# Causal attention in groups of four query tiles: values over up to 512 columns, a written TensorE order, value halves added on GpSimd

## The chip, the core and the metric

One core of a Trainium2 chip runs the whole program; the other cores are idle. The metric is the device time of one execution in microseconds (us), and lower is better. A time is the median over several executions.

Engines are named as in the profile: PE is TensorE (matmuls and transposes), PEld its weight loads, DVE is VectorE, ACT is ScalarE, POOL is GpSimd, SP is the engine that issues DMAs. Each takes its instructions in the order in which they stand in its own queue, and waits on semaphores that other engines raise.

## The reference

The program is one layer of a decoder: a gated feed-forward half step, three mixing branches, an output projection, and a second feed-forward half step, over 1024 tokens of width 1024 in float32. Only the middle branch is touched, a causal attention with 8 heads, queries and keys of 96 features (64 plain and 32 rotated) and values of 64:

```python
def causal_block_attention(q, k, v):              # q, k: (1, 1024, 8, 96), v: (1, 1024, 8, 64)
    ...
    def one_block(args):                          # Q_BLOCK = 128 queries at a time
        i, qi = args
        s = jnp.einsum('bqhd,bkhd->bhqk', qi, k).astype(jnp.float32) * scale
        qpos = i * Q_BLOCK + jnp.arange(Q_BLOCK)
        mask = kpos[None, :] <= qpos[:, None]
        s = jnp.where(mask[None, None], s, NEG)
        p = jax.nn.softmax(s, axis=-1)
        return jnp.einsum('bhqk,bkhd->bqhd', p.astype(v.dtype), v)
```

## The kernel before

Products are made from float32 values that are kept as two parts, a high part (`hi`, fp32r) and a rest (`lo`). `split` makes them: ACT copies the value to `hi` (L139), then DVE subtracts `hi` from the value to get `lo` (L142). `mm3` (L155) multiplies two such pairs with three matmuls (L158, L159, L160).

`attention` (L941) works on tiles of 128 queries by 128 keys. Head `h` has 8 query tiles, taken in four steps `j` of two tiles (`t` = 0, 1). Four kinds of work make a head:

- `prepare(h)` brings queries and keys to a layout with features on the partitions: four transposes of 128x96 (L450) into one PSUM bank, then ACT with a gain (L150) and DVE for the rest (L151). Four such pieces a head are spread over the steps of the head before.
- `scores(h, j)`: for each of two query tiles, three matmuls for each 512 columns of keys into a PSUM tile `mm` (two of these exist, of two banks each); DVE adds the causal mask and takes the row's extreme in one instruction (L1001, followed by a small read of the accumulator), writing the tile `pr0` to `pr7` that belongs to the query tile; ACT takes the exponential and its row sum (L1007).
- `turn(h, j)`: PE transposes the 128x128 blocks of `pr` (L1023) into a bank, four to a bank, and `split` makes `whi` and `wlo` from the bank. Blocks above the diagonal that a value product needs are cleared by POOL (L1028).
- `value(h, j)`: for each block row of keys `kk`, two matmuls over 256 columns (L1039 with `whi`, L1040 with `wlo`) into one bank. The stationary operand is `vv[kk]`, which holds the 64 high and the 64 low columns of the values side by side, so the bank's upper 64 rows and lower 64 rows are two halves of the result that have to be added: ACT copies one half (L1047), DVE adds the other (L1048) into `ysum`.

After two heads a 512-column piece of `ysum` is complete. The row sums' reciprocals (L1051) go to DRAM and come back spread over 64 partitions (L1066, L1068), POOL multiplies (L1071), and `split` writes the result to `yt` for the branch product that follows. For the last head PE transposes do that spreading instead of the DMAs (L1061).

The loop over steps runs `scores` of step n, then `turn` of step n-1, then `value` of step n-2. No order is written by hand in this stage: a scheduler puts the recorded instructions on each engine's queue. There are four PSUM banks of 512 columns (`bank`) for transposes and value sums together; `wide` tiles (`whi`, `wlo`) have five buffers each. `products` are matmuls of another branch that fill the start of the stage.

Of the kernel before, what the change touches and what calls it, by code (L numbers as in the profile page):

```python
# [8 lines left out]
F32 = mybir.dt.float32  # L9
# [4 lines left out]
ALU = mybir.AluOpType  # L14
AXX = mybir.AxisListType.X

P = 128
# [32 lines left out]
class Kernel:  # L50
# [890 lines left out]
    def attention(self, products):  # L941
# [16 lines left out]
        yt, st, qkt, pair, ysum, inv, late = [], {}, {}, {}, {}, {}, []  # L958
        sums = self.dram.tile([H // 2, 2, 2, 4 * P], F32, name="invd")
        with tc.tile_pool(name="att", bufs=1) as p:  # L960
# [21 lines left out]
            def scores(h, j):  # L982
                qt, kt = qkt[h]
                prs = []
                if h % 2 == 0 and j == 0:
                    inv[h // 2] = self.small.tile([P, 2, NT], F32, name="a_rs", tag="a_rs")
                rs = inv[h // 2][:, h % 2, 2 * j:2 * j + 2]
                mx, = (self.stat(x, 2) for x in ("a_mx",))
                ns = []
                for t in range(2):  # L990
                    i = 2 * j + t
                    n = {0: 256, 4: 768}.get(i, (i + 1) * P)
                    sc = self.mm().rearrange("p a b -> p (a b)")
                    for c0 in range(0, n, 512):
                        c = slice(c0, min(n, c0 + 512))
                        self.mm3(
                            sc[:, c], tuple(x[:, i * P:(i + 1) * P] for x in qt),
                            tuple(x[:, c] for x in kt), True, True)
                    pr = p.tile([P, (i + 1) * P], F32, name=f"pr{i}", bufs=1)
                    m, m0 = (i + 1) * P, (NT - 1 - i) * P  # L1000
                    nc.vector.tensor_tensor_reduce(  # L1001
                        out=pr[:, :m], in0=sc[:, :m], in1=self.mask[:, m0:m0 + m], scale=1.0, scalar=-NEG,
                        op0=ALU.add, op1=ALU.min, accum_out=mx[:, t:t + 1])
                    ns.append(m)
                    prs.append(pr)
                for t, (pr, n) in enumerate(zip(prs, ns)):
                    nc.scalar.activation(  # L1007
                        pr[:, :n], pr[:, :n], ACT.Exp, bias=mx[:, t:t + 1], scale=-1.0, accum_out=rs[:, t:t + 1])
                st[h, j] = prs

            def turn(h, j):
                prs, out = st[h, j], []
# [1331 lines left out]
```

## Time and profile before

| | |
|---|---|
| median of 3 runs | 2162.41 us (2160.59 to 2163.39) |
| the profiled execution | 2161.68 us, of which the span of its instructions is 2160.0 us |
| PE, PEld, DVE, ACT, POOL busy, whole span | 100%, 83%, 73%, 42%, 12% |
| granted PE clock | 1.00 |
| the attention stage, about 1240 to 1400 us | of 160 us PE is busy 158.59, DVE 138.78, ACT 130.61, POOL 28.04 |
| DMA in that stretch | 0.25 of its time, 78 GB/s |

Matmuls are pipelined: the profile gives one a duration that reaches into the next, so the busy share of PE hides short waits, and the cost of a matmul in a stream is read from start to start. On the other engines an instruction's start to the next one's start is also a little less than its duration, where they follow without a wait.

### The profile page before, as it was taken

To read this page: it belongs to the slowest core of one execution; us is meant where nothing else is said; L and a number is where in the kernel's file an instruction comes from. 1 tells how busy PE (TensorE), PEld (TensorE's weight loads), DVE (VectorE), ACT (ScalarE), POOL (GpSimd) and SP (SyncE) were. 2 spreads that over 40 slices of the span, in tenths; PEclk is the share of its full clock that TensorE was granted. 3 is DMA by queue.
4 is the path that set the end of the run, shared out by engine and by line. 5 is a ranking of instruction groups with operands and counts; after the bars stand their busy time and mean duration, and the time that the engine had idled before them with its cause. 6 is when DMAs were issued, how large, how long until landed. Compare 5 with 4: busy or idle time off the path is not lost.

```text
span 2160.0 us, 27488 instructions
## 1 busy us (share of the span) xinstructions
PE 2150.9 (100%) x10112; PEld 1797.1 (83%) x10112; DVE 1568.7 (73%) x2370; ACT 909.4 (42%) x1485; POOL 253.2 (12%) x256
## 2 busy tenths in 40 slices
PE   9999999999999999999999999999999999999999
PEld 6888888888888888888888899888888888888887
DVE  8966666679889657654886689886876666657884
ACT  6433333343455334433555378733433223224332
POOL 0011111100000000000123311230011212110000
PEclk9999999999999999999999999999999999999999
DMA  4264555585344444641687832292133332347543
GB/s 148 93 221 166 183 178 205 178 320 193 119 134 156 147 161 176 215 149 61 221 284 255 315 100 71 79 348 101 40 127 103 112 98 99 103 146 287 168 129 104
DMA packets 139751, 350.44 MB, mean 162 GB/s; under 512 B 21984, under 2 KB 30304, under 8 KB 139616
## 3 DMA queue, kind: packets, MB, share of 16 engines
q1 hardware_dynamic: 139472, 348.68, 46.9%
q8 instruction: 79, 1.29, 0.2%
q14 instruction: 56, 0.46, 0.1%
q10 hardware_dynamic: 144, 0.00, 0.0%
HBM read 235.62 MB, written 113.01 MB: 161 GB/s over the span
## 4 chain that ended last, share of the span: by engine, by line
PE 93%; DVE 4%; ACT 1%; DMA 1%; issue 0%; SPq 0%; POOL 0%; ACTq 0%; DVEq 0%; POOLq 0%
PE one L158 15%; PE one L159 15%; PE one L160 15%; PE bank L159 13%; PE bank L158 13%; PE bank L160 13%; PE mm L158 1%; PE mm L159 1%; PE mm L160 1%; PE bank L1023 1%; PE one L1979 1%; PE bank L1039 1%; DVE pr L1001 1%; PE bank L1040 1%; PE bank L1979 0%; DMA whi<-wks 0%
## 5 line engine op out<-in xcount | busy, mean ns | idle before, releaser
L146 ACT CAST whi<-x 128x1024 fp32r<-128x1024 f32 x202 | 192.2, 954 | 405.6 <-DVE x L1449 160.8
L147 DVE TENSOR_TENSOR wlo<-x,whi 128x1024 fp32r<-128x1024 f32 x202 | 237.3, 1176 | 70.1 <-DMA wkv<-wlo 24.6
L1483 DVE TENSOR_TENSOR t<-t,one 128x512 f32<-128x512 f32 x188 | 129.0, 686 | 184.7 <-PE one L160 182.3
L158 PE MATMUL bank<-h,whi 128*128 128x512 f32 x636 | 248.0, 390 | 0.0
L160 PE MATMUL bank<-h,wlo 128*128 128x512 f32 x636 | 247.7, 389 | 0.0
L159 PE MATMUL bank<-h,whi 128*128 128x512 f32 x636 | 247.6, 389 | 0.0
L158 PE MATMUL one<-h,whi 128*128 128x512 f32 x508 | 198.5, 391 | 0.0
L160 PE MATMUL one<-h,wlo 128*128 128x512 f32 x508 | 197.7, 389 | 0.0
L159 PE MATMUL one<-h,whi 128*128 128x512 f32 x508 | 197.7, 389 | 0.0
L158 PE MATMUL one<-w,whi 128*128 128x512 f32 x432 | 168.7, 391 | 0.2 <-DVE t L1483 0.2
L160 PE MATMUL one<-w,wlo 128*128 128x512 f32 x432 | 168.2, 389 | 0.0
L159 PE MATMUL one<-w,whi 128*128 128x512 f32 x432 | 168.2, 389 | 0.0
L142 DVE TENSOR_TENSOR wlo<-w,whi 128x1024 fp32r<-128x1024 f32 (+2 forms) x112 | 114.5, 1038 | 65.8 <-ACT whi L139 65.6
L139 ACT CAST whi<-w 128x1024 fp32r<-128x1024 f32 (+2 forms) x112 | 98.8, 900 | 148.7 <-PE one L159 63.9
L2079 POOL TENSOR_TENSOR raw<-raw 128x512 f32<-128x512 f32 x38 | 56.9, 1498 | 795.4 <-DVE raw L1920 703.5
L160 PEld LDWEIGHTS bank<-h,wlo 128*128 128x128 f32 x636 | 119.4, 188 | 24.9
L159 PEld LDWEIGHTS bank<-h,whi 128*128 128x128 f32 x636 | 119.4, 188 | 24.6
L158 PEld LDWEIGHTS bank<-h,whi 128*128 128x128 f32 x636 | 119.4, 188 | 24.5
L158 PE MATMUL bank<-whi 128*128 128x512 f32 x352 | 137.0, 389 | 0.0
L160 PE MATMUL bank<-whi,wlo 128*128 128x512 f32 x352 | 137.0, 389 | 0.0
L159 PE MATMUL bank<-wlo,whi 128*128 128x512 f32 x352 | 137.0, 389 | 0.0
L158 PEld LDWEIGHTS one<-h,whi 128*128 128x128 f32 x508 | 95.4, 188 | 19.8 <-issue 0.2
(406 smaller groups left out, 4892.7 us busy)
## 6 DMA issues: line engine op xcount, KB each, us to landing
x<-in_ffn_w_gu_dram SPq DMA_DIRECT2D x78, 512.0 KB, 5.1
w<-tdt SPq DMA_DIRECT2D x40, 512.0 KB, 4.3
gate<-raw SPq DMA_DIRECT2D x33, 512.0 KB, 2.9
tdb<-raw SPq DMA_DIRECT2D x64, 256.0 KB, 2.5
h<-in_ffn_w_down_dram SPq DMA_DIRECT2D x64, 256.0 KB, 6.0
w<-tdb SPq DMA_DIRECT2D x30, 512.0 KB, 4.5
tdt<-w SPq DMA_DIRECT2D x48, 256.0 KB, 2.6
x<-in_w_gate_dram SPq DMA_DIRECT2D x22, 512.0 KB, 6.9
```

What stands on the lines that cost most here:

```text
L139: i = self.nc.scalar.copy(hi, src)
L142: return (eng or self.nc.vector).tensor_tensor(lo, src, hi.bitcast(F32), op=ALU.subtract)
L146: self.nc.scalar.copy(hi, src)
L147: return lambda: self.nc.vector.tensor_tensor(lo, src, hi.bitcast(F32), op=ALU.subtract)
L158: i = mmul(out, s[0], m[0], start=first, stop=False, **kw)
L159: mmul(out, s[0], m[1], start=False, stop=False, **kw)
L160: self.last = mmul(out, s[1], m[0], start=False, stop=last, **kw)
L1001: nc.vector.tensor_tensor_reduce(out=pr[:, :m], in0=sc[:, :m], in1=self.mask[:, m0:m0 + m], scale=1.0, scalar=-NEG, op0=ALU.add, op1=ALU.m ...
L1023: nc.tensor.transpose(b[:, at:at + P], prs[t][:, kk * P:(kk + 1) * P], self.ident)
L1039: nc.tensor.matmul(o, w, pt[0], start=n == 0, stop=False)
L1483: return self.nc.vector.tensor_tensor(out, x, y, op=ALU.add)
L2079: sub = lambda d, x, y: (eng or nc.gpsimd).tensor_tensor(d, x, y, op=ALU.subtract)
```

## The change

The query tiles are taken in two groups `g` of four (tiles 0 to 3 and 4 to 7) rather than in four steps of two.

- `scores(h, i)` handles one query tile; the matmuls are the same.
- `turn(h, g, kk)` transposes the blocks of one block row of keys for all four query tiles of the group and splits them: as many transposes as before (36 a head), in 12 banks a head instead of 10. POOL clears 4 blocks a head instead of 8.
- `value(h, g, kk)` multiplies by up to 512 columns: for group 0 512, 384, 256, 256 columns, for group 1 five times 512, then 384, 256, 256, each twice (`hi`, `lo`): 24 matmuls a head instead of 40. The sum of a group stays in its bank from the first block row to the last.
- `close`: for all heads but the last, ACT copies the whole bank (128x512) to a row tile, a DMA brings the other 64 rows to `ysum`'s partitions, and POOL adds. The second half of the final split is on POOL too. The last head keeps the path over ACT and DVE.
- `cycle(h)` writes out PE's order. R is a piece of `prepare` for the next head, S a query tile's scores, N one of the next head, T a turn, V a value; A is the head's own group 0, B is group 1 of the head before.
- PE's order is now the order of recording (`manual_schedule`). The queues of DVE, ACT, POOL and SP are still ordered by the scheduler.

```diff
+            def turn(h, g, kk):
+                if kk % 2 == 0:
+                    pts[h, g] = [self.wide(n).rearrange("p (c q) -> p c q", c=2) for n in ("whi", "wlo")]
+                hi, lo = (x[:, kk % 2] for x in pts[h, g])
+                b, z = self.bank(), max(0, kk - 4 * g)
+                for t in range(z, 4):
+                    nc.tensor.transpose(b[:, t * P:(t + 1) * P], st[h, 4 * g + t][:, kk * P:(kk + 1) * P], self.ident)
+                at = min(z, 2) * P
+                z *= P
+                if at < z:
+                    for x in (hi, lo):
+                        nc.gpsimd.memset(x[:, at:z].bitcast(F32), 0.0)
+                self.split(hi[:, z:], lo[:, z:], b[:, z:])
+                pts[h, g, kk] = at, hi[:, at:], lo[:, at:]
...
-                    nc.tensor.matmul(o, w, pt[0], start=n == 0, stop=False)
-                    nc.tensor.matmul(o, w, pt[1], start=False, stop=n == len(pts) - 1)
+                for k, x in enumerate(pt):
+                    nc.tensor.matmul(
+                        o[:, at:], w, x, start=kk == k == 0, stop=kk == 4 * g + 3 and k == 1, skip_group_check=True)
...
-                nc.scalar.copy(y, o[other])
-                nc.vector.tensor_tensor(y, y, o[rows], op=ALU.add)
+                if h == H - 1:
+                    nc.scalar.copy(ys[rows], o[other])
+                    nc.vector.tensor_tensor(ys[rows], ys[rows], o[rows], op=ALU.add)
+                else:
+                    both = self.row()
+                    nc.scalar.copy(both, o)
+                    nc.sync.dma_start(ys[rows], both[other])
+                    nc.gpsimd.tensor_tensor(ys[rows], ys[rows], both[rows], op=ALU.add)
...
-                        self.split(y[0][:, cols], y[1][:, cols], ys)
+                        self.split(y[0][:, cols], y[1][:, cols], ys, None if end else nc.gpsimd)
...
+                return [
+                    *R(2), *TB(0, 1), *S(4), *VB(0, 1), *TB(2, 3, 4), *S(5), *VB(2, 3, 4), *TB(5, 6, 7), *S(6), *VB(5, 6, 7),
+                    *R(1), *TA(0, 1), *S(7), *VA(0, 1), *R(1), *TA(2, 3), *N(0, 1), *VA(2, 3), *N(2, 3)]
+
+            ahead = [prepare(h) for h in range(H)]
+            next(ahead[0])
+            with tc.manual_schedule(engines={mybir.EngineType.PE}):
+                for _ in range(4):
+                    next(ahead[0], None)
                     next(products)
...
+                for h in range(H + 1):
+                    if h + 1 < H:
+                        next(ahead[h + 1])
+                    for f, *x in cycle(h):
+                        f(*x)
```

The first place where the change moves instructions is PE's queue around the scores of query tile 7 (the six matmuls into one `mm` tile) in the fourth head. Before, L1023 are transposes, and L1039 and L1040 the value matmuls with `whi` and `wlo` (numbers tell buffers apart):

```order
L160 MATMUL mm_11367<-h4_11005,h4_11004 128x512
L450 MATMUL bank_11266<-ident_86,ak_11258 96x128 x4
L1023 MATMUL bank_11275<-ident_86,pr1_11188 128x128
L1023 MATMUL bank_11275<-ident_86,pr0_11182 128x128
L1023 MATMUL bank_11275<-ident_86,pr1_11188 128x128
L1039 MATMUL bank_11283<-whi_11192,h4_10302 128x256
L1040 MATMUL bank_11283<-wlo_11193,h4_10302 128x256
L1039 MATMUL bank_11283<-whi_11192,h4_10301 128x256
```

With the change the transposes are L1011 and the value matmuls L1027; the same six score matmuls write `mm_11302`:

```order
L1011 MATMUL bank_11289<-ident_86,pr3_11137 128x128
L1011 MATMUL bank_11296<-ident_86,pr1_11111 128x128
L1011 MATMUL bank_11296<-ident_86,pr2_11130 128x128
L1011 MATMUL bank_11296<-ident_86,pr3_11137 128x128
L158 MATMUL mm_11302<-h4_10908,h4_10906 128x512
L159 MATMUL mm_11302<-h4_10909,h4_10906 128x512
L160 MATMUL mm_11302<-h4_10908,h4_10907 128x512
L158 MATMUL mm_11302<-h4_10908,h4_10906 128x512
L159 MATMUL mm_11302<-h4_10909,h4_10906 128x512
L160 MATMUL mm_11302<-h4_10908,h4_10907 128x512
L1027 MATMUL bank_11312<-whi_11287,h4_10301 128x512
L1027 MATMUL bank_11312<-wlo_11288,h4_10301 128x512
```

Before, the scores are followed by seven transposes and then 16 value matmuls whose operands (`whi_11192`, `wlo_11193`) come from a turn one step back; now the value matmuls right behind the scores read the tiles (`whi_11287`, `wlo_11288`) that are split from the transposes just ahead of the scores.

The second place is DVE's queue for the same head. In it "ISA pr7" is the masked reduction of query tile 7 (with the accumulator's read behind it), L142 the subtraction that makes a `wlo`, L151 that of `prepare`. Before:

```order
L142 TENSOR_TENSOR wlo_11193<-bank_11201,whi_11192 128x512
L142 TENSOR_TENSOR wlo_11209<-bank_11210,whi_11208 128x512
L1001 ISA pr6_11365,a_mx_11357<-mm_11358,mask_10353 128x896
L1001 ISA a_mx_11357 128x1
L142 TENSOR_TENSOR wlo_11209<-bank_11217,whi_11208 128x384
L1048 TENSOR_TENSOR ysum_11238<-ysum_11238,bank_11225 64x256
L1001 ISA pr7_11374,a_mx_11357<-mm_11367,mask_10353 128x1024
```

And with the change (L998 is the masked reduction; `pr0` and `pr1` belong to the next head):

```order
L998 ISA pr7_11309,a_mx_11180<-mm_11302,mask_10353 128x1024
L998 ISA a_mx_11180 128x1
L142 TENSOR_TENSOR wlo_11288<-bank_11289,whi_11287 128x512
L142 TENSOR_TENSOR wlo_11288<-bank_11296,whi_11287 128x384
L1048 RECIPROCAL a_inv_11511<-a_rs_10862 128x8
L998 ISA pr0_11343,a_mx_11338<-mm_11339,mask_10353 128x128
L998 ISA a_mx_11338 128x1
L151 SCALAR_TENSOR_TENSOR h4_11147<-bank_11317,a_gq_10358,h4_11146 96x512
L998 ISA pr1_11350,a_mx_11338<-mm_11346,mask_10353 128x256
L998 ISA a_mx_11338 128x1
L142 TENSOR_TENSOR wlo_11325<-bank_11326,whi_11324 128x256
L142 TENSOR_TENSOR wlo_11325<-bank_11331,whi_11324 128x128
```

Before, the subtractions for the values that follow the scores of tile 7 stand ahead of that tile's reduction; now the reduction of tile 7 stands ahead of the subtractions of `wlo_11288`, and those of the next head's tiles 0 and 1 ahead of the subtractions of `wlo_11325`.

The third place is ACT's queue at the turn from this head to the next. Before (L1007 is the exponential, L1047 the copy of half a value bank, L139 the copies to `whi`):

```order
L1007 ACTIVATE pr0_11441,a_rs_11435<-pr0_11441,a_mx_11436 128x128
L139 CAST whi_11392<-bank_11394 128x512
L1007 ACTIVATE pr1_11447,a_rs_11435<-pr1_11447,a_mx_11436 128x256
L139 CAST whi_11392<-bank_11401 128x512
L139 CAST whi_11408<-bank_11410 128x384
L1007 ACTIVATE pr2_11504,a_rs_11435<-pr2_11504,a_mx_11499 128x384
L1047 COPY ysum_11099<-bank_11418 64x256
L1007 ACTIVATE pr3_11510,a_rs_11435<-pr3_11510,a_mx_11499 128x512
L139 CAST whi_11451<-bank_11453 128x512
```

With the change L1001 is the exponential, L1043 the copy of a whole value bank, L150 the gain of `prepare`; `whi_11399` belongs to the first two turns of group 1:

```order
L1001 ACTIVATE pr1_11350,a_rs_11337<-pr1_11350,a_mx_11338 128x256
L1043 COPY t_11357<-bank_11312 128x512
L1001 ACTIVATE pr2_11371,a_rs_11337<-pr2_11371,a_mx_11338 128x384
L150 ACTIVATE h4_11383<-bank_11385,g_ev_k_3345 96x512
L1001 ACTIVATE pr3_11378,a_rs_11337<-pr3_11378,a_mx_11338 128x512
L139 CAST whi_11399<-bank_11401 128x512
L150 ACTIVATE h4_11381<-bank_11392,a_gq_10358 96x512
L139 CAST whi_11399<-bank_11408 128x512
L139 CAST x4_10672<-ysum_11118 128x512
L139 CAST whi_11431<-bank_11433 128x512
```

Before, copies of a turn stand between the exponentials of tiles 0 to 3; now the copies to `whi_11399`, the next ones, stand behind all of these exponentials and alternate with two pieces of `prepare`; `x4_10672` is the copy of a finished `ysum` piece, which POOL has to deliver.

More of the change, by code (lines that the diff above doesn't have):

```diff
@@ L980, in prepare, with scores @@
                             gain[n])
-            def scores(h, j):
+            def scores(h, i):
                 qt, kt = qkt[h]
-                prs = []
-                if h % 2 == 0 and j == 0:
+                if h % 2 == 0 and i == 0:
                     inv[h // 2] = self.small.tile([P, 2, NT], F32, name="a_rs", tag="a_rs")
[L987 to L1009, printed above, removed]
@@ new lines, in scores @@
+                n, m, m0 = {0: 256, 4: 768}.get(i, (i + 1) * P), (i + 1) * P, (NT - 1 - i) * P
+                sc = self.mm().rearrange("p a b -> p (a b)")
+                for c0 in range(0, n, 512):
+                    c = slice(c0, min(n, c0 + 512))
+                    self.mm3(
+                        sc[:, c], tuple(x[:, i * P:(i + 1) * P] for x in qt),
+                        tuple(x[:, c] for x in kt), True, True)
+                pr = p.tile([P, m], F32, name=f"pr{i}", bufs=1)
+                t = mx[0][:, i % 4:i % 4 + 1]
@@ L1049, in value @@
-                if h % 2 and j % 2:
+                if h % 2 == 0:
+                    ysum[h // 2, g] = p.tile([P, 4 * P], F32, name="ysum", bufs=3)
+                ys = ysum[h // 2, g]
+                if h == H - 1:
[6 more added lines that the diff above has]
+                    nc.gpsimd.tensor_tensor(ys[rows], ys[rows], both[rows], op=ALU.add)
@@ new lines, in close, with cycle @@
+                    late.append((0 if end else 3, scale))
+            def cycle(h):
+                S = lambda *ts: [(scores, h, i) for i in ts if h < H]
+                N = lambda *ts: [(scores, h + 1, i) for i in ts if h + 1 < H]
+                R = lambda n: [(next, ahead[h + 1], None) for _ in range(n) if h + 1 < H]
+                step = lambda f, h, g, ks: [(f, h, g, k) for k in ks if 0 <= h < H]
+                TB, VB = (lambda *ks, f=f: step(f, h - 1, 1, ks) for f in (turn, value))
+                TA, VA = (lambda *ks, f=f: step(f, h, 0, ks) for f in (turn, value))
+                return [
+                    *R(2), *TB(0, 1), *S(4), *VB(0, 1), *TB(2, 3, 4), *S(5), *VB(2, 3, 4), *TB(5, 6, 7), *S(6), *VB(5, 6, 7),
+                    *R(1), *TA(0, 1), *S(7), *VA(0, 1), *R(1), *TA(2, 3), *N(0, 1), *VA(2, 3), *N(2, 3)]
@@ new lines, in attention @@
+            ahead = [prepare(h) for h in range(H)]
[3 more added lines that the diff above has]
+                    next(ahead[0], None)
+                    next(products)
+                for i in range(4):
+                    scores(0, i)
+                next(products, None)
+                for h in range(H + 1):
[3 more added lines that the diff above has]
+                        f(*x)
+                        if f is value and x[2] in (3, 7):
+                            late = [(d - 1, f) for d, f in late]
+                            while late and late[0][0] < 0:
+                                late.pop(0)[1]()
```

83 lines of the change are left out of this document (24 added, 59 removed).

## The prediction

> **What bounds the kernel now.** I read the page first, then the attention stage alone (busy time by stretch, PE's waits, the instructions in order of time, the groups by shape).
>
> ```profile
> span 2160.0 us, 27488 instructions
> PE 2150.9 (100%) x10112; PEld 1797.1 (83%) x10112; DVE 1568.7 (73%) x2370; ACT 909.4 (42%) x1485; POOL 253.2 (12%) x256
> PE 93%; DVE 4%; ACT 1%; DMA 1%; issue 0%; SPq 0%; POOL 0%; ACTq 0%; DVEq 0%; POOLq 0%
> ```
>
> The chain that ended last is PE for 93%. The change touches one stage, so what counts is whether PE is the limit there too:
>
> ```profile
> 1240.00:1400.00 160.00, 158.59 (x1110) 144.95 (x1109) 138.78 (x301) 130.61 (x290) 28.04 (x77) 1.00 0.25 78
> ```
> ```profile
> PE bank L1039 <- DVE ysum L1048: 0.6, 2, 0.5
> PE bank L1039 <- DVE wlo L142: 0.3, 1, 0.3
> PE bank L1023 <- DVE wlo L142: 0.2, 1, 0.2
> ```
>
> In these 160 us PE is idle for 1.4 (160 - 158.59), and the three waits that have a name are 1.1 of it. But DVE is busy for 138.8 and ACT for 130.6: what PE turns and multiplies has passed through both, and only the distance in the queues between a turn and the values that read it hides that. PE's own prices are read from start to start:
>
> ```profile
> 1299.70 0.42 PE L158 MATMUL mm<-h,h 96*128 96x384 f32 x1
> ...
> 1307.23 0.34 PE L159 MATMUL mm<-h,h 96*128 96x384 f32 x1
> ...
> 1307.59 0.28 PE L1039 MATMUL bank<-whi,h 128*128 128x256 f32 x1
> ...
> 1309.02 0.40 PE L158 MATMUL mm<-h,h 96*128 96x512 f32 x1
> ...
> 1310.41 0.60 PE L450 MATMUL bank<-ident,ak 128*96 128x128 f32 x4
> 1310.85 0.49 PE L1023 MATMUL bank<-ident,pr 128*128 128x128 f32 x3
> ...
> 1317.20 0.42 PE L158 MATMUL mm<-h,h 96*128 96x384 f32 x1
> ```
>
> A 384-column matmul takes 0.18 us ((1307.59 - 1307.23)/2), a 256-column one 0.119 (twelve in 1307.59 to 1309.02), a 512-column one 0.232 (six in 1309.02 to 1310.41), a transpose 0.11 (0.44/4). The first and last rows are the same matmul of two heads in a row: a head takes 17.5 us.
>
> **What the change takes away.** Before, a head has 40 value matmuls of 256 columns: 320 x 0.119 = 38.1 us. After, 24: 12 of 512, 4 of 384, 8 of 256 columns, over 8 heads 96 x 0.232 + 32 x 0.18 + 64 x 0.119 = 35.7. That is 2.4 us less, all of it on PE's path. Scores, transposes and `prepare` are as many as before. If the written order left no wait at all, the 1.4 us of idle would go too: 3.8 us is the most that can be won here.
>
> DVE loses the half additions and a subtraction (some 4 x 0.415 + 0.68 us a head, rows below), ACT trades four half copies for two whole ones and has two more banks to copy. Relief of DVE pays only if DVE's load were the bound; PE is, so I count nothing for it. Four fewer clearings on POOL: nothing.
>
> **What the change adds: waits of PE for tiles just turned.** Values now read what was transposed one score product earlier, and the queues of DVE and ACT have other work between. The prices:
>
> ```profile
> 1310.61 1.23 DVE L1001 CUSTOM_DVE_ANT_0 pr<-mm,mask 128x1024 f32<-128x1024 f32 x1 [0.58 <-PE mm L160]
> ...
> 1311.77 0.75 DVE L151 SCALAR_TENSOR_TENSOR h<-bank,g_ev_k,h 96x512 fp32r<-96x512 f32 x1
> ```
> ```profile
> 1389.35 1.29 DVE L142 TENSOR_TENSOR wlo<-bank,whi 128x512 fp32r<-128x512 f32 x2 [0.70 <-issue]
> ...
> 1390.10 0.38 PE L1039 MATMUL bank<-whi,h 128*128 128x256 f32 x1 [0.33 <-DVE wlo L142]
> ```
> ```profile
> L142 DVE TENSOR_TENSOR wlo<-bank,whi 128x512 fp32r<-128x512 f32 x42 | 28.2, 678 | 0.2 <-ACT whi L139 0.2
> L142 DVE TENSOR_TENSOR wlo<-bank,whi 128x384 fp32r<-128x384 f32 x27 | 14.7, 545 | 0.0
> L1048 DVE TENSOR_TENSOR ysum<-ysum,bank 64x256 f32<-64x256 f32 x27 | 11.2, 415 | 3.0 <-ACT ysum L1047 2.5
> L151 DVE SCALAR_TENSOR_TENSOR h<-bank,g_ev_k,h 96x512 fp32r<-96x512 f32 x13 | 9.6, 742 | 0.4 <-ACT h L150 0.3
> L1001 DVE CUSTOM_DVE_ANT_0 pr<-mm,mask 128x512 f32<-128x512 f32 x7 | 4.7, 673 | 0.0
> L1001 DVE DVE_READ_ACCUMULATOR2_ANT a_mx<- 128x1 f32 x58 | 4.6, 79 | 0.0
> L1001 DVE CUSTOM_DVE_ANT_0 pr<-mm,mask 128x256 f32<-128x256 f32 x7 | 2.9, 414 | 0.0
> L1001 DVE CUSTOM_DVE_ANT_0 pr<-mm,mask 128x128 f32<-128x128 f32 x7 | 2.0, 283 | 0.1
> L139 ACT CAST whi<-bank 128x512 fp32r<-128x512 f32 x42 | 23.7, 575 | 1.3 <-PE bank L1023 1.0
> L1047 ACT COPY ysum<-bank 64x256 f32<-64x256 f32 x27 | 9.9, 366 | 3.2 <-PE bank L1040 2.5
> L150 ACT ACTIVATE h<-bank,g_ev_k 96x512 fp32r<-96x512 f32 x13 | 8.9, 683 | 2.1 <-PE bank L450 1.9
> L1007 ACT ACTIVATE pr<-pr,a_mx 128x512 f32<-128x512 f32 x7 | 5.1, 725 | 0.2
> L1007 ACT ACTIVATE pr<-pr,a_mx 128x384 f32<-128x384 f32 x7 | 4.4, 622 | 0.0
> ```
>
> DVE begins 0.20 us after PE has gone on from the last score matmul (1310.61 - 1310.41), its next instruction starts 1.16 after the reduction of tile 7 (1311.77 - 1310.61), and PE starts 0.06 after the subtraction it waits for (the first of two begun at 1389.35, 0.68 long, ends 1390.03; PE 1390.10).
>
> (a) *Values of group 0 behind the scores of tile 7.* In heads 2 to 7 DVE's queue has the reduction of tile 7 ahead of both subtractions. So the second value matmul cannot start before 0.20 + 1.16 + 0.68 + 0.06 = 2.10 us after the scores end, and PE has one 512-column matmul, 0.23, for that time: a wait of 1.87. In heads 1 and 8 only the second subtraction (0.545) stands behind the reduction: 0.20 + 1.16 + 0.545 + 0.06 = 1.97, against 2 x 0.232 + 0.18 = 0.64: 1.33. Sum 6 x 1.87 + 2 x 1.33 = 13.9. Before, this reduction passed unseen: 7 transposes and 16 value matmuls of an older turn followed the scores.
>
> (b) *The other two values of group 0.* From the end of (a) PE has `prepare` 0.44, three transposes 0.33, the next head's tiles 0 and 1 0.71: 1.48, then the values. In five heads DVE does the reduction of tile 0, the piece of `prepare`, the reduction of tile 1, and then the subtraction. ACT ends its part of `prepare` at 0.64 + 0.68 = 1.32, DVE the first reduction at 1.6, `prepare` at 2.3, the second reduction at 2.7, the subtraction (256 columns: between the rows 0.415 and 0.545, nearer the first since its columns are as many, 0.42) at 3.1; the matmul that could start at 1.60 starts at 3.15: 1.55. At least 0.98 of it is fixed by the order alone (1.48 + 0.20 + 0.42 + 0.42 + 0.06 - 1.60). In the other three heads the subtraction stands ahead of the reductions: 0.9. Sum 5 x 1.55 + 3 x 0.9 = 10.4.
>
> (c) *The first two values of group 1.* Count from the end of the next head's tile 3. PE has `prepare` 0.88, eight transposes 0.88, scores 1.05, and is at the first value at 2.81. ACT's queue: exponential of tile 2, `prepare`, exponential of tile 3 (about 1.4 to 2.1), copy (to 2.7), `prepare` (3.3), copy (3.8). DVE: subtraction to 3.4, `prepare` to 4.05, subtraction to 4.7. PE's four matmuls then end at 4.98 and not at 3.74: 1.2 us, seven times: 8.4. It could be 0, if ACT and DVE run ahead after the waits of (b), or 2, if they are late.
>
> (d) *The end.* In the last group nothing stands between turns and values. A block takes 0.20 + 0.575 + 0.68 + 0.06 and a hand-over, about 1.55, from its transposes to its `lo` matmul, against cover by PE's own work of 0.67, 1.1 and 0.5 in the three rounds; in the second, subtractions at 0.68 against pairs of matmuls at 0.46 add some, in the third the blocks are smaller: 0.9 + 0.7 + 0.7 = 2.3. Heads' group 1 in the middle (blocks 2 to 7) have scores between, and by the same walk no wait.
>
> (e) *The halves over DMA and POOL.* No row shows this chain; the nearest are:
>
> ```profile
> L1071 POOL TENSOR_TENSOR ysum<-ysum,t 128x512 f32<-128x512 f32 x6 | 7.7, 1288 | 39.7 <-DVE ysum L1048 25.1 <-PE bank L1023 8.7 <-PE bank L1039 6.0
> t<-invd SPq DMA_DIRECT2D x12, 128.0 KB, 3.6
> ```
>
> From a finished value bank: copy 0.58, DMA as large as this one 3.6, addition and multiplication 1.29 each, 6.8 us until ACT's queue may copy the piece. It reaches that copy about 5 us after the bank is finished, six times, and the next copies of a turn stand behind it: six times 1.8 us at worst, 10.8; nothing, where PE is waiting for something else. PE has slack of 1 to 1.5 us at these places, so I take 0.5 each: 3. On SP's queue 14 such DMAs stand between those of the row sums, which have a head's time: nothing. The buffer of the clearing for the last value of group 0 waits on POOL behind an addition, some 2 us before PE asks for it: nothing.
>
> Does GpSimd's added work slow DVE?
>
> ```profile
> 1232.98 2.38 DVE L142 TENSOR_TENSOR wlo<-raw,whi 128x512 fp32r<-128x512 f32 x2
> 1233.15 1.67 POOL L574 TENSOR_TENSOR x<-x,x 128x512 f32<-128x512 f32 x1
> ```
> ```profile
> 1287.16 1.29 POOL L1071 TENSOR_TENSOR ysum<-ysum,t 128x512 f32<-128x512 f32 x1 [6.78 <-DVE ysum L1048]
> 1287.86 0.08 DVE L1001 DVE_READ_ACCUMULATOR2_ANT a_mx<- 128x1 f32 x1
> 1287.86 0.69 DVE L142 TENSOR_TENSOR wlo<-bank,whi 128x512 fp32r<-128x512 f32 x1
> ```
>
> Two subtractions with both operands in SBUF took 2.38 us beside POOL, where two of 0.68 would be 1.4; one that reads a bank took 0.69 beside POOL. All of DVE's operations in this stage read a bank, so I take 0. The Trainium skill (GPSIMD Engine Reference, Specifications) says that the SBUF interfaces are shared with VectorE, with contention for DVE instructions in a 2-port mode or with two SBUF inputs: by that the sum is the same 0; by the plainer statement of one shared interface it would be some 1 us on DVE for each of 20 added POOL operations (14 additions, 6 subtractions), 20 us. The trace agrees with the first.
>
> **Sum.** 13.9 + 10.4 + 8.4 + 2.3 + 3 = 38.0 of new waits, less 3.8: +34.2. The profiled execution took 2161.68 us (span 2160.0), 0.73 under the median of 2162.41; 2161.68 + 34.2 = 2195.9, so 2196.
>
> **Rivals.**
> - *Only the fixed part (same sign):* (c) and (e) hide behind the waits of (a) and (b), and (b) is 0.98: 13.9 + 5 x 0.98 + 3 x 0.5 + 2.3 - 3.8 = +18.8, 2180.5. For it: PE's waits let ACT and DVE catch up. It lies inside the range.
> - *Faster:* the stage is held by DVE's load (138.8 of 160 busy), and the order in which DVE has its work is of no weight because subtractions come early enough. Then the stage falls by PE's 3.8: 2157.9. It decides if DVE's reduction of tile 7 costs PE under 0.5 us a head (8 x 0.5 = 4). Against it: the reduction needs scores that end just ahead of the waiting values.
> - *No change:* waits of about 3.8 in all, under 0.5 a head: 2162. Same objection.
> - *Much slower:* the chain of (e) holds ACT for its full 10.8, and with it every value behind; or DMA waits grow to the longest seen. 2196 + 8 to 2196 + 25: 2204 to 2221.
> - *PE's clock falls with the new waits.* The granted clock is 1.00 in the row above, with no wait over 0.5 us in it, so this trace cannot tell. At half clock in half the stage: +70, 2266. The Trainium skill (TensorE: Matmul & The Clock Gate, Part 1: The HAM clock gate) has the clock halved after an idle window of 3.4 us; the longest wait forecast here is under 2, so by that page it stays.
>
> **How the numbers follow.** The forecast (2174 to 2210, the fixed part included) has 0.86, faster 0.04, no change 0.02, much slower beyond 2210 0.06, the clock 0.02. The range runs from what (a) and the order's share of (b) give alone (13.9 + 4.9 - 3.8: 2176.7) and a little under, to (c) at 2 us and (e) at 10 us (+5.6 and +7.8). About 0.2%, 4 us, is what a measurement can tell here. So faster 0.04, same 0.02, slower 0.94.
>
> **What would show it.** In the changed kernel's trace: PE's waits by name, with the value matmuls (L1027) waiting for DVE's subtraction (L142) some 30 us in all; behind the scores of tile 7 a gap of almost 2 us in every head; value matmuls 24 a head with 512 columns at 0.232; the time from one head to the next up from 17.5 to about 21.5 us; PE idle some 35 to 40 us between 1240 and 1435. Wrong it would be if DVE's reductions start well before the scores' neighbours on PE end, if the gap behind tile 7 is under 0.5 us, or if the largest waits are for POOL or a DMA.

## The result, and the profile after

The changed kernel takes 2213.13 us (median of 6 runs, 2210.45 to 2215.64), the kernel before 2161.32 in the same comparison (2159.34 to 2163.39): 1.0241 times as long, 95% interval 1.0231 to 1.0251, or 51.8 us more. The forecast was 34 more, 2196, with a range to 2210; the direction was right, the size was not.

The page after: span, busy engines, the chain that ended last; then the attention stage as one stretch (us, then PE, PEld, DVE, ACT, POOL busy, granted clock, DMA share, GB/s), and PE's waits in it (us in total, times, longest):

```profile
span 2210.9 us, 27223 instructions
PE 2175.1 (98%) x9984; PEld 1798.6 (81%) x9984; DVE 1557.5 (70%) x2350; ACT 907.5 (41%) x1485; POOL 272.6 (12%) x244
PE 92%; DVE 3%; DMA 2%; ACT 1%; issue 1%; POOL 1%; SPq 0%; POOLq 0%; ACTq 0%; DVEq 0%
```
```profile
1240.00:1450.00 210.00, 181.49 (x977) 145.06 (x976) 127.99 (x281) 127.74 (x289) 49.31 (x71) 0.94 0.24 70
```
```profile
PE bank L1027 <- DVE wlo L142: 19.1, 29, 1.3
PE bank L1027 <- ACT whi L139: 8.2, 13, 3.2
PE mm L158 <- DVE a_mx L998: 0.3, 1, 0.3
```

PE is idle for 28.5 us of these 210 (210 - 181.49), where it was 1.4 of 160 before, and its granted clock is 0.94, where it was 1.00. The waits have the names that were forecast: value matmuls (L1027) for tiles just turned, most of them for DVE's subtraction. Two things were not forecast: one wait of 3.2 us for ACT, and the clock.

The wait behind the scores of tile 7 in the second head, in order of time, on PE and on DVE:

```profile
1284.36 0.39 PE L160 MATMUL mm<-h,h 96*128 96x512 f32 x1
1284.93 0.50 PE L1027 MATMUL bank<-whi,h 128*128 128x512 f32 x1 [0.18 <-ACT whi L139]
1286.68 0.51 PE L1027 MATMUL bank<-wlo,h 128*128 128x512 f32 x1 [1.25 <-DVE wlo L142]
```
```profile
1284.79 1.23 DVE L998 CUSTOM_DVE_ANT_0 pr<-mm,mask 128x1024 f32<-128x1024 f32 x1 [0.63 <-PE mm L160]
1285.94 1.15 DVE L142 TENSOR_TENSOR wlo<-bank,whi 128x512 fp32r<-128x512 f32 x2
```

DVE takes the reduction of tile 7 first, both subtractions after it, as in the prediction. From the last score matmul to the second value matmul PE uses 1286.68 - 1284.36 = 2.32 us, of which 2 x 0.229 is streaming: 1.86 of wait, where 1.87 was forecast. It is 1.86 or 1.87 in all of heads 2 to 7.

The one long wait, at 1302, followed back: SP's queue, the transfer's time to landing (from the chain, start and duration), GpSimd, ACT, PE:

```profile
1287.56 0.37 SPq L1063 DMA_DIRECT2D invd<-a_inv  x1
1291.79 0.48 SPq L1044 DMA_DIRECT2D ysum<-t  x1
```
```profile
1291.79 6.59 DMA ysum<-t
```
```profile
1298.54 1.26 POOL L1045 TENSOR_TENSOR ysum<-ysum,t 64x512 f32<-64x512 f32 x1 [11.97 <-DMA ysum<-t]
1299.88 1.26 POOL L1068 TENSOR_TENSOR ysum<-ysum,t 128x512 f32<-128x512 f32 x1
1301.18 0.62 ACT L139 CAST x<-ysum 128x512 fp32r<-128x512 f32 x1 [5.91 <-POOL ysum L1068]
1302.33 0.49 PE L1027 MATMUL bank<-whi,h 128*128 128x512 f32 x1 [3.23 <-ACT whi L139]
```

ACT's queue has the first copy of the finished piece (x<-ysum) ahead of the copies of a turn. It stood idle for 5.91 us until GpSimd had added and multiplied, and GpSimd had waited for a transfer that took 6.59. That is the chain (e) of the prediction with its longest link longer than allowed for.

The clock, in stretches of 3.41 us (same columns as above; PE's busy time is the first number behind the comma, the clock the third from the end). They come in pairs, each with the stretch behind it:

```profile
1309.59:1313.01 3.42, 2.12 (x10) 1.21 (x8) 2.51 (x5) 2.61 (x6) 1.27 (x2) 1.00 0.65 152
1313.01:1316.42 3.41, 2.69 (x17) 2.17 (x17) 1.42 (x5) 2.57 (x7) 2.60 (x3) 1.00 0.59 207
...
1333.49:1336.90 3.41, 1.98 (x11) 1.36 (x11) 2.50 (x5) 1.85 (x4) 1.41 (x2) 1.00 0.01 4
1336.90:1340.31 3.41, 2.42 (x17) 2.02 (x16) 1.83 (x7) 2.46 (x8) 0.00 (x0) 1.00 0.34 40
...
1377.86:1381.27 3.41, 1.98 (x9) 1.00 (x7) 2.64 (x5) 2.61 (x6) 1.41 (x2) 1.00 0.18 38
1381.27:1384.69 3.42, 3.42 (x16) 3.11 (x15) 0.91 (x4) 1.54 (x6) 0.00 (x0) 0.50 0.24 40
...
1405.17:1408.58 3.41, 1.98 (x9) 1.04 (x8) 2.30 (x4) 2.27 (x6) 2.25 (x3) 1.00 0.22 62
1408.58:1411.99 3.41, 2.79 (x14) 2.49 (x12) 1.43 (x6) 2.22 (x7) 1.79 (x2) 0.50 0.00 0
1411.99:1415.41 3.42, 3.16 (x10) 2.77 (x11) 0.96 (x4) 1.65 (x5) 0.00 (x0) 0.50 0.09 21
1415.41:1418.82 3.41, 3.41 (x15) 3.12 (x14) 2.17 (x5) 1.92 (x6) 2.30 (x5) 0.50 0.08 17
```

The clock is 1.00 or 0.50 for a whole stretch, and the stretches lie on one grid (from the first slow one at 1302.77 to the one at 1398.34 are 28 times 3.413 us). Seven stretches in the stage are at half clock, 23.9 us, in five groups; each group follows a stretch in which PE was busy for 2.01 us or less. Of the other stretches only the one at 1333.49 was that low.

To have terms that can be compared, I read PE's starts from the first transpose of the stage to the last value matmul, take the price of each matmul off (0.229, 0.176, 0.119, 0.109), and sort what is left: in a slow stretch up to one more price goes to the clock, more than 0.15 us is a wait, the rest small gaps.

| kernel | stage | waits | longer at half clock | small gaps |
|---|---|---|---|---|
| before | 153.6 | 2.7 | 0 | 2.8 |
| changed | 206.6 | 40.3 | 10.1 | 8.6 |

The stage is 53.0 us longer, and twelve 512-column matmuls of other work (2.7 us) have moved into it, which leaves 50.3; the spans differ by 50.9.

### The profile page after: what moved, and what is told of

Its sections match the earlier page's. It is cut to its first block, busy times and chain, and to the rows that moved or that the text cites. A ratio compares the mean times of both kernels' runs of the same rounds, so it can differ in the third digit from the quotient of the medians.

```text
span 2210.9 us, 27223 instructions
## 1 busy us (share of the span) xinstructions
PE 2175.1 (98%) x9984; PEld 1798.6 (81%) x9984; DVE 1557.5 (70%) x2350; ACT 907.5 (41%) x1485; POOL 272.6 (12%) x244
## 4 chain that ended last, share of the span: by engine, by line
PE 92%; DVE 3%; DMA 2%; ACT 1%; issue 1%; POOL 1%; SPq 0%; POOLq 0%; ACTq 0%; DVEq 0%
PE one L158 15%; PE one L159 15%; PE one L160 15%; PE bank L158 13%; PE bank L159 13%; PE bank L160 13%; PE bank L1027 2%; PE mm L158 1%; PE mm L159 1%; PE mm L160 1%; PE bank L1011 1%; DMA ysum<-t 1%; DVE wlo L142 1%; PE one L1982 1%; PE bank L1982 0%
## 5 line engine op out<-in xcount | busy, mean ns | idle before, releaser
L142 DVE TENSOR_TENSOR wlo<-w,whi 128x1024 fp32r<-128x1024 f32 (+2 forms) x112 | 114.4, 1037 | 65.4 <-ACT whi L139 65.1
L139 ACT CAST whi<-w 128x1024 fp32r<-128x1024 f32 (+2 forms) x112 | 98.8, 902 | 150.1 <-PE one L159 63.9
L160 PEld LDWEIGHTS one<-h,wlo 128*128 128x128 f32 x508 | 95.6, 188 | 20.0
```

The costliest lines, as they stand in the source:

```text
L139: i = self.nc.scalar.copy(hi, src)
L142: return (eng or self.nc.vector).tensor_tensor(lo, src, hi.bitcast(F32), op=ALU.subtract)
L160: self.last = mmul(out, s[1], m[0], start=False, stop=last, **kw)
```

## The experiments

All are set against runs of the kernel before on the same chip; the ratio stands with its 95% interval.

**1. VectorE keeps the written order** (dve_order)

```
-            with tc.manual_schedule(engines={mybir.EngineType.PE}):
+            with tc.manual_schedule(engines={mybir.EngineType.PE, mybir.EngineType.DVE}):
```

> VectorE, too, keeps the written order in the attention stage, so both subtractions of group 0 stand ahead of the reduction of tile 7, and those of tiles 2 and 3 ahead of the next head's reductions. Theory (order and clock: the new time is some 40 us of waits, (a) 14, (b) 10, (c) 6, (d) 3, (e) 7, and some 12 us of matmuls at half clock in the 3.41 us windows that follow a window in which PE was busy under about 0.6): (a) falls to 2 to 4, (b) to about 3, and the windows at half clock behind them go: 11 + 7 + 7 = 25 less, 2188 (2180 to 2196). Rival (halves: what the forecast missed is the path over DMA and GpSimd alone, and the waits for VectorE are those for late data): under 5 less, 2208 to 2213. Rival (clock costs nothing): 18 less, 2195.

Measured: 2273.46 us, 1.0516 (1.0500 to 1.0532): 60 us slower than the changed kernel, which no theory had. PE's waits, ACT's for the piece, and SP's queue at the place of the rows above:

```profile
PE bank L1027 <- ACT whi L139: 31.8, 12, 8.3
PE bank L450 <- DMA aq<-qd: 17.9, 2, 9.4
PE bank L1027 <- DVE wlo L142: 15.9, 22, 2.0
```
```profile
ACT x L139 <- POOL ysum L1068: 62.3, 7, 11.6
```
```profile
1294.32 0.38 SPq L1063 DMA_DIRECT2D invd<-a_inv  x1
1294.86 0.47 SPq L1044 DMA_DIRECT2D ysum<-t  x1
1305.63 1.10 SPq L1065 DMA_DIRECT2D t<-invd  x2
```

The part that was meant came true: with the subtractions ahead of the reduction, the wait behind tile 7's scores in the second head is 0.34 + 0.55 us, no longer 1.86. But the reciprocals of the row sums now stand at their written place too. In the changed kernel the one for group 0 of the second head was on its way at 1272.5; here its write starts at 1294.32, SP goes on only when it has landed, 11.29 us later, the multiplication waits for that, and ACT's queue for the multiplication: 62.3 us where it was 15.9 in the changed kernel:

```profile
ACT x L139 <- POOL ysum L1068: 15.9, 6, 5.9
```

PE also waits up to 9.4 us for the next queries' transfer. So this does not measure the gain of the order alone; it shows what ACT's queue behind the piece can cost.

**2. The halves added by VectorE again** (halves_dve)

```
-                if h == H - 1:
+                if True:
                     nc.scalar.copy(ys[rows], o[other])
                     nc.vector.tensor_tensor(ys[rows], ys[rows], o[rows], op=ALU.add)
...
-                        self.split(y[0][:, cols], y[1][:, cols], ys, None if end else nc.gpsimd)
+                        self.split(y[0][:, cols], y[1][:, cols], ys)
```

> One part undone: in all heads ACT copies one half and VectorE adds the other from the bank, and the last subtraction is VectorE's again; no transfer between halves, no GpSimd addition. Theory (order and clock): the waits of (e), 7, and the two windows at half clock behind them, 3, go; VectorE gets 13 additions and 6 subtractions of about 0.69, 13 us more, which give some back: 2204 (2199 to 2211). Rival (halves): 17 or more less, 2196 or under. Rival (VectorE's load is the limit): slower than 2213.

Measured: 2199.67 us, 1.0178 (1.0163 to 1.0193): 13.5 less than the changed kernel, just inside the theory's range. The waits for ACT (8.2, longest 3.2) are down to 2.9, those for DVE stay:

```profile
PE bank L1027 <- DVE wlo L142: 17.7, 28, 1.1
PE bank L1027 <- ACT whi L139: 2.9, 9, 0.5
```

So the path over DMA and GpSimd costs over a quarter of the 51.8; by itself it is not the cause of the rest, and VectorE takes back 12 us of work (busy for 1569.7 us against 1557.5) without showing it.

**3. The halves alone, in the old order** (old_gp)

```
-                nc.scalar.copy(y, o[other])
-                nc.vector.tensor_tensor(y, y, o[rows], op=ALU.add)
...
+                    both = self.row()[:, :2 * P]
+                    nc.scalar.copy(both, o)
+                    nc.sync.dma_start(y, both[other])
+                    nc.gpsimd.tensor_tensor(y, y, both[rows], op=ALU.add)
...
-                        self.split(y[0][:, cols], y[1][:, cols], ys)
+                        self.split(y[0][:, cols], y[1][:, cols], ys, None if last else nc.gpsimd)
```

The last head keeps its old path here too.

> The other part alone: the kernel before, in its own order and with values of 256 columns, but the halves go over a DMA and a GpSimd addition, and the last subtraction of a pair is GpSimd's. Theory (order and clock): the chain has a whole head's time here before ACT copies the piece, nobody waits: 2161 (2158 to 2166). Rival (halves): it costs what it costs in the changed kernel, 10 to 17: 2171 to 2178.

Measured: 2161.10 us, 0.9999 (0.9989 to 1.0008). The same path with twice the transfers costs nothing where the order gives it a head's time: ACT still waits for GpSimd's piece four times there, 6.1 us in all, but PE's waits in the stage are only 1.6 us (1.1 before). So what the path costs in the changed kernel comes from the order around it; whether that is the place of ACT's copy in its queue is the next experiment.

**4. Where the path costs: ACT's queue** (x_pool)

```
-                        self.split(y[0][:, cols], y[1][:, cols], ys, None if end else nc.gpsimd)
+                        if end:
+                            self.split(y[0][:, cols], y[1][:, cols], ys)
+                        else:
+                            nc.gpsimd.tensor_copy(y[0][:, cols], ys)
+                            nc.gpsimd.tensor_tensor(y[1][:, cols], ys, y[0][:, cols].bitcast(F32), op=ALU.subtract)
```

> Halves still over DMA and GpSimd, but the first copy of the finished piece is GpSimd's, not ACT's, so nothing in ACT's queue waits for the piece; GpSimd gets six copies of a microsecond more. Theory (the cost of the halves is ACT's queue held behind the piece): the waits of (e), 7 to 9, and the stretches at half clock behind them, 3, go, and VectorE has no additions: 2201 (2197 to 2205). Rival (the cost is GpSimd's own, its buffers or the clearings behind the additions): 2210 or more.

Measured: 2199.31 us, 1.0179 (1.0165 to 1.0193): 13.8 less, as in experiment 2 and inside the theory's range, though here transfers and additions stay as they were, and three transfers are still late (6.19, 3.48 and 5.58 us from issue to landing, the others 2.2 to 2.6).

```profile
PE bank L1027 <- DVE wlo L142: 18.3, 26, 1.3
PE bank L1027 <- ACT whi L139: 1.7, 8, 0.4
```

That settles it: GpSimd may be late; what costs is ACT's copy of a late piece ahead of the copies that PE waits for.

**5. Why the transfer is late: SP's queue?** (act_queue)

```
-                    nc.sync.dma_start(ys[rows], both[other])
+                    nc.scalar.dma_start(ys[rows], both[other])
```

> The changed kernel, with the transfers of halves issued on ACT's queue, no longer on SP's. In the trace of the changed kernel the transfers of the odd heads' group 0 landed 4.7 to 6.8 us after their issue, the others after 2.3 to 2.5; those three alone stand on SP's queue behind the write of the reciprocal sums (4 KB in 4-byte pieces, landing 9 us after its issue). Theory (a transfer lands no earlier than one ahead of it on the same queue): now all land after about 2.4, ACT's queue is released 2 to 4 us earlier at three places, (e) falls from 7 to about 2: 2206 (2202 to 2210). Rival (those transfers are late for another reason, such as what else moves then): 2213, within 3.

Measured: 2215.30 us, 1.0244 (1.0230 to 1.0258): no better, as the rival has it. In the changed kernel the three late transfers had landed after 6.59, 4.49 and 5.43 us and the other eleven after 2.2 to 2.4, a little earlier than the figures above; here the same three took 7.14, 4.59 and 6.89. The transfer of the second head's group 0 is issued on another queue and is as late (issue on ACT's queue; GpSimd's addition; time to landing of all 14):

```profile
1289.74 0.47 ACTq L1044 DMA_DIRECT2D ysum<-t  x1
```
```profile
1297.04 1.26 POOL L1045 TENSOR_TENSOR ysum<-ysum,t 64x512 f32<-64x512 f32 x1 [12.05 <-DMA ysum<-t]
```
```profile
DMA to landing us min/median/max: 2.2/2.3/7.1
```

My theory of one queue falls in that form. In both traces the write of the reciprocals is under way at this time (changed kernel: issued 1287.56, landed 1297.28; here 1286.00 and 1295.52), and what was issued behind it, on whichever queue, landed after it: the two reads of an older write, issued at 1288.03 and 1288.62, at 1297.97 and 1298.17, the half of 1291.79 at 1298.38. Of the half, the packets had moved by 1293.7. The same holds in each of the two traces for all nine transfers that were issued behind a write of reciprocals and well before its landing.

A wider theory fits what the traces show: a transfer lands no earlier than one issued ahead of it, on whichever queue. Of the pairs of transfers that were under way together in the whole program (2619 in the changed kernel, 2623 here, 24 of these on two engines' queues) not one landed out of the order of issue. It also explains two more late halves here, issued at 1307.65 and 1357.69, each 0.2 us behind the load of the next keys on SP's queue: they landed after 5.45 and 5.06 us, each just behind that load. Why the write itself takes so long to land was not tried with another form of it; its packets had moved 8 us before its landing (by 1289.2 in the changed kernel).

**6. The clock, measured by filling PE's wait** (fill_a, dve_fill, x_pool_fill: the same edit in the changed kernel, in halves_dve and in x_pool)

```
                 for k, x in enumerate(pt):
+                    for _ in range(6 if kk == k == g == 0 else 0):
+                        nc.tensor.matmul(o[:, at:], w, x, start=True, stop=False, skip_group_check=True)
                     nc.tensor.matmul(
```

> The first value matmul of group 0 (it starts the sum afresh) is written seven times instead of once, in every head: 6 x 0.232 = 1.39 us of work for PE inside the wait of 1.52 us of (a); nothing else begins earlier or later. Theory (order and clock): no window falls under 0.6 busy at these places, so the stretches at half clock from 1381, 1408 (10.24 us) and perhaps 1432 go, and about half of their length is won: 2206 (2203 to 2209). Rival (clock costs nothing, the slow stretches lie where PE waits anyway): 2213, within 2. Rival (the filling delays the value matmuls): 2215 or more.

> Halves added on VectorE as in halves_dve, and the first value matmul of group 0 written seven times in every head as in fill_a. In halves_dve PE had 17.1 us at half clock, all right behind the waits for tiles of group 0, and matmuls in it were 6.7 us longer than at full clock; the long waits for ACT, which moved about between the runs of the changed kernel and of fill_a, are gone here. Theory (clock: a window of 3.41 us in which PE is busy under 0.6 sets the next to half clock): with 1.4 us more work in the window the stretches go, and 5 to 7 us with them: 2194 (2192 to 2196). Rival (clock costs nothing): 2199.7, within 2. Rival (the filling delays): over 2201.

> As x_pool, with the first value matmul of group 0 written seven times in every head. In x_pool PE had four stretches of 3.41 us at half clock, in which matmuls were 5.8 us longer than at full clock. Theory (a stretch of one window is hidden: PE arrives later at its next wait for VectorE, and that wait is shorter by as much; only a stretch of two or three windows costs): all stretches go and the time stays: 2199 (2197.5 to 2200.5). Rival (the clock costs what its matmuls are longer): 2193.5. Rival (the filling delays): over 2201.

| kernel | us | ratio (interval) | at half clock | longer by it | from head to head, second to sixth |
|---|---|---|---|---|---|
| changed | 2213.13 | 1.0241 (1.0231 to 1.0251) | 23.9 | 10.1 | 26.5, 22.4, 23.2, 22.0, 26.9 |
| fill_a | 2210.15 | 1.0229 (1.0214 to 1.0245) | 13.7 | 4.8 | 28.0, 22.4, 23.3, 22.4, 27.5 |
| halves_dve | 2199.67 | 1.0178 (1.0163 to 1.0193) | 17.1 | 6.7 | 22.3, 22.1, 24.2, 22.2, 22.3 |
| dve_fill | 2197.79 | 1.0170 (1.0156 to 1.0184) | 0 | 0 | 22.3, 22.1, 22.3, 22.1, 22.3 |
| x_pool | 2199.31 | 1.0179 (1.0165 to 1.0193) | 13.7 | 5.8 | 22.1, 22.0, 23.0, 21.6, 23.1 |
| x_pool_fill | 2196.97 | 1.0161 (1.0147 to 1.0175) | 0 | 0 | 22.0, 22.0, 22.0, 22.0, 22.0 |

The last column is the time from the first value matmul behind tile 7's scores to that of the next head. In x_pool_fill the added matmuls and the wait:

```profile
1327.46 1.65 PE L1028 MATMUL bank<-whi,h 128*128 128x512 f32 x6 [0.16 <-ACT whi L139]
1328.96 0.39 PE L1029 MATMUL bank<-whi,h 128*128 128x512 f32 x1
1329.24 0.50 PE L1029 MATMUL bank<-wlo,h 128*128 128x512 f32 x1
```
```profile
1240.00:1430.00 190.00, 175.86 (x1003) 140.63 (x1002) 124.52 (x276) 122.60 (x280) 51.19 (x74) 1.00 0.24 69
```

The second value matmul starts 1.78 us after the first of the run, as before the filling (1.75), and the clock is 1.00 throughout: with 48 more matmuls no stretch falls low. So PE's idle share does set the clock. None of the three times lies in its theory's range: fill_a came out between its theory and the rival by which the clock costs nothing, dve_fill just inside that rival, x_pool_fill 0.5 under its theory. What the slow stretches cost lies between nothing and full price. Full price would have been 6.7 and 5.8 us; the medians fell by 1.9 and 2.3, and by 1.7 and 3.9 when each is taken by its ratio; the intervals of each pair overlap, so no single number is shown. In the profiled executions the stage alone, from first transpose to last value matmul, is 3.0 and 2.9 us shorter with the filling. The heads tell how it goes: in halves_dve a slow stretch of 6.8 us made one head 1.9 us longer, while those of 3.4 us at 1286.5 and 1354.8 made theirs 0.1 longer, since PE came later to its next wait and waited less, and the one at 1399.2 made its head, the seventh, 1.0 longer. In x_pool two of 3.4 us cost 1.0 and 1.1 us, and the head between them was 0.4 shorter. So the theory that a single stretch is hidden was too kind, and that it costs its matmuls' length too hard. In fill_a the slow stretches behind tile 7's scores went (17 of 24 us), but in its profiled execution the waits for ACT's queue at values 2 to 4 were 1.7 us longer, with two slow stretches of 6.8 us behind them in place of two of 3.4.

**7. Another written order** (far, far_dve, far_xpool, far3_xpool)

```
-   *R(2), *TB(0, 1), *S(4), *VB(0, 1), *TB(2, 3, 4), *S(5), *VB(2, 3, 4), *TB(5, 6, 7), *S(6), *VB(5, 6, 7),
-   *R(1), *TA(0, 1), *S(7), *VA(0, 1), *R(1), *TA(2, 3), *N(0, 1), *VA(2, 3), *N(2, 3)]
+   *R(2), *TB(0, 1), *S(4), *TB(2, 3, 4), *VB(0, 1), *S(5), *TB(5, 6, 7), *VB(2, 3, 4), *S(6), *TA(0, 1),
+   *VB(5, 6, 7), *S(7), *R(1), *TA(2, 3), *VA(0, 1), *R(1), *N(0, 1), *VA(2, 3), *N(2, 3)]
```

far_dve has the halves of experiment 2 with this order, far_xpool the copy of experiment 4; far3_xpool has in addition R(1) behind TB(0, 1), VB(2, 3, 4), VB(5, 6, 7) and S(7) in place of the four here.

> The changed kernel with another written order: each value run stands one turn run and one score product further behind its turns (turns 2 to 4 ahead of values 0 and 1, turns 5 to 7 ahead of values 2 to 4, the first turns of group 0 ahead of values 5 to 7, its last ahead of its first values); halves still over DMA and GpSimd. Theory (order and clock): (a) 14, (b) 10, (c) 6 fall to 3 or so together, the windows at half clock behind them go (5 to 7); (e) stays and may be smaller by the longer distance: 2213 - 27 - 6 = 2180 (2172 to 2188). Rival (VectorE or ACT has too much to do in the stage, whatever the order): over 2200.

> The order of far, and the halves added on VectorE. Theory (order, halves and clock are all there is): only the end (d), some 3 us, and small hand-overs are left; no window at half clock: 2164 (2158 to 2170), about the time before. Rival (VectorE's load): 2180 or more.

> The order of far, and GpSimd makes the first copy of the finished piece as in x_pool. In far 18.7 us of PE's waits were for ACT's queue held behind the piece, and 9.6 were lost at half clock behind them; in far_dve 8.3 us were for the value bank that VectorE's addition frees late, which the whole copy on ACT frees here. Theory (order, and ACT's queue held): both go, left are the transfer of the next queries (4.6) and the end: 2171 (2166 to 2177). Rival (GpSimd's or VectorE's load now sets the pace): 2185 or more.

> As far_xpool, with the four pieces of preparation of the next head spread over the order (behind the turns 0 and 1, behind values 2 to 4, ahead of the scores of tile 7 and behind them), so that some 1.5 us more lie between the last use of the queries' buffer and the first use of the next load. Theory: the waits for that load (4.6) go: 2166 (2160 to 2171). Rival (the pieces take banks and queue places from the turns): no better than far_xpool.

Measured: far 2207.04, 1.0211 (1.0197 to 1.0225); far_dve 2178.91, 1.0086 (1.0072 to 1.0100); far_xpool 2185.39, 1.0102 (1.0088 to 1.0116); far3_xpool 2174.49, 1.0056 (1.0042 to 1.0069). All four came out above my numbers; far and far_xpool lie where their rivals put them (over 2200, 2185 or more), but the waits do not have the names of those rivals, VectorE's or GpSimd's load. PE's waits in far, then in far3_xpool:

```profile
PE bank L1011 <- DVE wlo L142: 17.8, 3, 6.7
PE bank L450 <- DMA aq<-qd: 8.6, 3, 3.2
PE bank L1027 <- DVE wlo L142: 2.9, 4, 1.1
```
```profile
PE bank L1027 <- DVE h L151: 9.3, 7, 1.4
PE bank L1027 <- POOL whi L1016: 1.6, 2, 0.9
PE bank L1027 <- DVE wlo L142: 1.2, 2, 0.8
```

The values' waits for DVE's subtraction go as forecast, 19.1 to 2.9. But in far ACT's queue is held behind the piece all the more, 21.7 us against 15.9 (PE's three waits of up to 6.7 us are turns that want a bank which ACT and DVE have not emptied), and PE comes to the next queries before their transfer is in. In far_xpool that last wait stays, 8.5 us, with 17.1 us at half clock that make matmuls 6.3 us longer; in far_dve the largest wait is for a value bank that VectorE's addition frees late, 7.3. With the piece off ACT's queue and the transfer's time given back, what is left in far3_xpool is a value bank that a piece of preparation still holds, 9.3. Taking the order apart thus gave 25 of the 38 us that the changed kernel's other versions had left over the kernel before (2199.3 to 2174.5, with x_pool as the start), each time turning part of it into a wait with a new name. No version was faster than the kernel before.

## Why the prediction was wrong in size

By its own terms, against the changed kernel's trace (waits over 0.15 us):

| term | forecast | measured |
|---|---|---|
| (a) group 0 behind tile 7's scores | 13.9 | 13.95 |
| (b) the other two of group 0 | 10.4 | 10.2 |
| (c) first two of group 1 | 8.4 | 6.0 |
| (d) the end | 2.3 | 2.8 |
| (e) ACT held behind the piece | 3 | 7.35, and 13.8 with all that follows |
| PE's clock | 0 | 10.1 gross; of 6.7 and 5.8 gross 2 to 4 net where it could be isolated |

- (a) and (b), 24 us, are right to a few tenths in the sum, and in their cause: DVE does the reduction first. (b) has 1.4 us in it from ACT's queue, so the agreement of its sum is in part luck; single heads ran from 0.9 to 1.8. (c) was a little smaller, by a third, and one head less paid it.
- Of the signs, the gap behind tile 7's scores came as named. The profile's own idle time is less than forecast, 19.1 us of waits for DVE and 28.5 in all, where some 30 and 35 to 40 were named, since a matmul's duration reaches into the wait behind it; from start to start the waits that end with L142 come to 26.4 us and all waits to 40.3. A sign of being wrong came too: the longest wait, 3.2 us, hung on POOL and a DMA.
- x_pool_fill is the changed kernel without ACT's hold and without slow stretches: 34.8 us over the kernel before (2196.97 - 2162.20). The prediction without its 3 for (e) was 31.2 over it. In its own trace (a) to (d) come to 32.8, with the added matmuls counted as the wait that they fill, 2.2 less than forecast; gaps under 0.15 us, which no term had, are 7.5 more than before; and the kernel before had 2.7 of waits to lose, where 1.4 was taken off: 31.2 - 2.2 + 7.5 - 1.3 = 35.2. From head to head it is 22.0 there, where 21.5 was forecast.
- The step that failed is (e). Its chain, its place and its end in ACT's queue were named; the size was not. I took the transfer at 3.6 us from a row of before and slack of 1 to 1.5 us at these places, and dismissed SP's queue ("which have a head's time: nothing") by asking only whether the new transfers hold up those of the row sums. It is the other way round: a transfer that was issued behind the write of the sums landed only after it, 6.6 us from its issue in place of 2.3 (experiment 5). Three waits at values 2 to 4 of group 1 came to 3.9, 1.2 and 2.2 us, not six of 0.5. With the slow stretches behind them, 13.8 us hang on that queue place (experiment 4), over 10 more than the 3 allowed for: that alone takes 2196 to 2207. What the late transfer costs by itself, apart from the copy's place in ACT's queue, no run shows. My upper end had room for 10.8 in (e) (the +7.8; the 10 beside it is a slip) but none for what it triggers.
- Of the other 6 us, 2 to 4 are the clock behind the waits that remain, and the rest are small gaps. The clock was a rival, which had 0.02 and a price of 70. I gave it little because the trace of before had no wait to show it, and no wait over 2 us was forecast. The Trainium skill (TensorE: Matmul & The Clock Gate, Part 1: The HAM clock gate) has the clock fall after an idle window of some 3.4 us, the windows running free. The trace agrees with windows of 3.41 us on a fixed grid and with the half clock; it disagrees with a wholly idle window as the condition: PE busy for 1.74, 1.98 and 2.01 of 3.41 us was enough. One such window that holds the whole wait (a) is at the bound, so the forecast of (a) was a forecast of slow stretches, had the bound been known.
- The rivals "only the fixed part", "faster" and "no change" fell with (a) and (b) as forecast. "Much slower" had the right chain and the right time, 2204 to 2221, at 0.06: ACT was held behind the piece for 15.9 us, more than the 10.8 called the worst, and 7.35 of it reached PE.
- What the sum takes off, the shorter streaming of the values, shows nowhere by itself; nothing speaks against it. The price of a 512-column value matmul is as forecast, and DVE's relief was worth nothing: halves_dve gives the work back and is no slower than x_pool.

## What to carry to other kernels

When work moves to a slower path, look at which in-order queue holds the instruction that consumes its result, and at what stands behind it there: the path may be late for free (old_gp), or cost 14 us through six copies of 0.62 us that stand in the wrong place. Of a transfer, ask what was issued ahead of it on any queue. When waits are forecast, add them up by windows of a few microseconds and not only one by one, since they can set the clock; then count of the slower matmuls only the part that the next wait does not take back. And an order written for one engine is an order for all the engines that feed it: check each queue's rows, and the transfers, before moving steps further apart.

## What the runs showed of the hardware that was not expected

- PE's granted clock falls to half for whole stretches of 3.413 us on a fixed grid. In the attention stage of every run here, a stretch at half clock followed either one in which PE was busy for 0.59 of the time or less (0.13, 0.51, 0.58, 0.58, 0.59 in the changed kernel) or another one at half clock. The bound is not sharp: a stretch at 0.58 (from 1333.49) was followed by full clock, and in far one at 0.41 (1.42 of 3.42 us, from 1364.65). Once slow, stretches at 0.82 and 0.92 were followed by another slow one (from 1408.58), and one at 0.93 by full clock (from 1302.77); in far_xpool one at 0.84 was followed by full clock (from 1271.81).
- A 4 KB write in 4-byte pieces took 8.2 to 10.5 us to land, before as after, and transfers issued meanwhile landed only behind it, on SP's queue as on ACT's: 6.6 and 7.1 us for a transfer of 128 KB that takes 2.3 otherwise. Transfers landed in the order of their issue throughout, over both queues: none of 2619 and 2623 overlapping pairs was out of order (experiment 5).
